# Second attention layer: where the transposed meta probabilities and the query norm sums live in PSUM

## The chip, the cores and the metric

One core of a Trainium2 chip. The metric is the device time of one execution in microseconds; lower is better. The kernel before was timed three times: 2624.48, 2630.35 and 2631.34 us, median 2630.35 us.

## The reference

A two-layer encoder over two sequences ("prompt" and "sample") of 512 tokens with 1024 features; 16 learned meta tokens are put in front of each, so that every sequence has 528 rows. Layer 0 is a gated DeltaNet mixer, layer 1 an attention mixer with compressed queries and keys (MLA). The change lies in layer 1:

```
proj = RMSNorm(h) @ w_in                      # cq 512 | ckv 256 | k_pe 64 | z 2048
q  = RMSNorm(cq)  @ w_uq   -> 16 heads x (128 + 64)
kv = RMSNorm(ckv) @ w_ukv  -> 16 heads x (128 key + 128 value)
q, k = RMSNorm per head over 192, then rotary on the last 64
p = softmax(q k^T / sqrt(192))                # over all 528 keys, the 16 meta keys among them
h = h + (p v * silu(z)) @ w_out               # meta rows dropped from the output
```

All arithmetic is in float32.

## The kernel before

**Arithmetic.** TensorE multiplies rounded operands. Each float32 matrix is split into a high part H (a cast) and a low part L (what the cast lost), and a product is three matmuls, H·H, H·L, L·H (`mm3`, lines 74 to 79; in the trace their lines are L75, L76, L77). The cast is a ScalarE instruction, the subtraction for L is VectorE's or GpSimd's (`sub`, L88). For the 16 meta tokens the three products are folded into one matmul: 80 rows hold H at 0 to 15, a second operand's H at 32 to 47 and L at 64 to 79. These stacked tiles are `pst` (probabilities, two tiles, one per head of a pair) and `vst` (values).

**Work units of layer 1.** 2 sequences x 8 head pairs make 16 units. A unit's preparation (`head`, in the order `pair_k`, `pair_qrope`, `pair_qsplit`, `pair_q` for head 0, `pair_v`, `pair_q` for head 1, `pair_z`) is issued as filling between the tiles of the unit before. Each unit then has 8 attention tiles: 2 heads x 4 query tiles of 128 rows. In `run` the loop over n issues, for each tile, one piece of the next unit's preparation, then `pair_scores` of the next tile, then `pair_out` of this tile.

- `pair_scores` writes 128x528 scores into a PSUM tile S (two banks, two such tiles), VectorE takes the maximum (L1089), ScalarE the exponential (L1093) into P (two SBUF tiles), VectorE scales P (L1096).
- `pair_out` transposes P on TensorE: its 16 meta columns (L1108) into the first 16 partitions of the second bank of S, which is then no longer needed for scores, and its other 512 columns (L1110) into the one `tr` bank. ScalarE copies the meta block twice into pst (L1113, L1114), VectorE subtracts (L88); ScalarE and VectorE split the 512 columns into PTH and PTL (in the trace hnH and hnL, whose memory they use). Query tiles go in pairs: only after the odd one are the output matmuls issued, for 256 columns, into a bank `x`: 12 with the 512 keys' values (L75 to L77), then one with the meta tokens (L1124). VectorE multiplies the result by the gate zs (L1125).
- `pair_q` (L1000 and on) projects the queries of one head, splits them (ScalarE L1009, VectorE qL L1012), and adds up their squares on ScalarE, GpSimd and VectorE (L1011, L1014, L1015). For head 1 it then sums them over the features by four small matmuls (L1020) into a tile of `x`, which VectorE reads (L1022). The key norm sums in `pair_k` (L993) are alike, in a projection bank `pj`.

**PSUM** has eight banks: S 2 x 2, `pj` 2, `tr` 1, `x` 1. A tile is given to its next user when all accesses to it are over.

**Order.** Each engine takes its instructions in order. That order is not the program's text: a list scheduler with a timeline simulation (`schedule_with_timeline_sim=True`) takes, at each step of its simulated time, the ready instruction that stands first in the program, and hands out tiles and semaphores as it goes. Weights are loaded by DMAs of the SP queue.

Of the kernel before, what the change touches and what calls it, by code (L numbers as in the profile page):

```python
# [18 lines left out]
NM = 16  # L19
# [4 lines left out]
class Trunk:  # L24
# [975 lines left out]
    def pair_q(self, u, j):  # L1000
        nc = self.nc
        V, A, G, PE = nc.vector, nc.scalar, nc.gpsimd, nc.tensor
        UQ, cq, sqr, h = self.ins["mla_w_uq"][0], u["c"]["cq"], u["sqr"], u["hs"][j]
        o = self.SIDES[j][0]
        w = self.weights([(0, UQ[:, 192 * h:192 * h + 128])], 4)
        ps = self.project(w, cq, 4, 0, 512)
        qH = self.t("qH", [128, 512], F32R)
        qL = self.t("qL", [128, 512], F32R)
        A.activation(qH, ps, AF.Copy, scale=self.qkg)  # L1009
        sq = self.t("raw", [128, 512])  # L1010
        A.activation(sq, ps, AF.Square)  # L1011
        V.scalar_tensor_tensor(qL, ps, self.qkg, qH.bitcast(F32), op0=ALU.mult, op1=ALU.subtract)  # L1012
        u["q"][j] = qH, qL
        G.tensor_tensor(sqr[o], sqr[o], sq[o], op=ALU.add)  # L1014
        V.tensor_tensor(sqr[o], sqr[o], sq[self.SIDES[j][1]], op=ALU.add)  # L1015
        if j == 0:
            return
        ps = self.p("x", [128, 4, 2])
        for i in range(4):
            PE.matmul(ps[:, i], sqr[:, 128 * i:128 * i + 128], self.two, start=True, stop=True)  # L1020
        t = self.t("qs", [128, 4, 2])
        V.tensor_tensor(t, ps, u["c"]["ce"].unsqueeze(2).to_broadcast([128, 4, 2]), op=ALU.add)  # L1022
        tf = t.rearrange("p a b -> p (a b)")
        self.rsqrt(tf, tf)
        u["qs"] = [t[:, :, j] for j in range(2)]
# [73 lines left out]
    def pair_out(self, u, j, qt, S, P):  # L1099
        nc = self.nc  # L1100
        V, A, G, PE = nc.vector, nc.scalar, nc.gpsimd, nc.tensor
        VH, VL, vst, zs = u["VH"], u["VL"], u["vst"], u["zs"][j]
        pst = self.pst[j]
        vc = slice(128 * j, 128 * j + 128)
        cs = slice(128 * qt, 128 * qt + 128)
        pt = self.p("tr", [128, 4, 128])
        pm = S[0:16, 1, 0:128]
        PE.transpose(pm, P[:, 0:NM], self.ident)  # L1108
        for kt_ in range(4):
            PE.transpose(pt[:, kt_], P[:, NM + 128 * kt_:NM + 128 * kt_ + 128], self.ident)  # L1110
        PTH, PTL = self.PT[qt // 2]
        hc = slice(128 * (qt % 2), 128 * (qt % 2) + 128)
        A.copy(pst[0:16, cs], pm)  # L1113
        A.copy(pst[32:48, cs], pm)  # L1114
        self.sub(V, pst[64:80, cs], pm, pst[0:16, cs])
        A.copy(PTH[:, :, hc], pt)  # L1116
        self.sub(V, PTL[:, :, hc], pt, PTH[:, :, hc])
        if qt % 2 == 0:
            return
        po = self.p("x", [128, 256])  # L1120
        h2 = slice(128 * qt - 128, 128 * qt + 128)
        for kt_ in range(4):
            self.mm3(po, (VH[:, kt_, vc], VL[:, kt_, vc]), (PTH[:, kt_], PTL[:, kt_]), first=(kt_ == 0), last=False)
        PE.matmul(po, vst[:, vc], pst[:, h2], start=False, stop=True)  # L1124
        V.scalar_tensor_tensor(zs[:, h2], po, 0.5, zs[:, h2], op0=ALU.mult, op1=ALU.mult)  # L1125
        if qt == 3:
            nc.sync.dma_start(u["yd"][u["hs"][j]], zs)
# [204 lines left out]
```

## Time and profile before

| | |
|---|---|
| median of three runs | 2630.35 us |
| profiled execution, its own time | 2632.01 us |
| its span, first to last instruction | 2630.3 us |
| mean granted TensorE clock | 0.97 of full speed |
| TensorE busy (matmul) | 2468.7 us, 94% |
| VectorE busy | 1732.9 us, 66% |
| ScalarE busy | 1408.4 us, 54% |
| GpSimd busy | 1166.6 us, 44% |

The profile is one execution. "Busy" of TensorE is the time in which at least one matmul is under way; matmuls overlap, so it is not peak use. The first layer takes the span up to some 1340 us; the attention tiles of the second run from 1540 to 2480 us; the output projection of the last sequence ends the span.

### The profile page before, as it was taken

Reading aid. Unit: us, or ns where it says so; the run is one execution under the profiler, and the core shown is the slowest. Engines: PE = TensorE matmul, PEld = TensorE weight load, DVE = VectorE, ACT = ScalarE, POOL = GpSimd, SP = SyncE. Lnnn points to the kernel's source line nnn. Section 1 sums busy time; section 2 is a strip of 40 time slices with the busy share of each in tenths; the row PEclk is TensorE's granted clock in tenths of the full one; section 3 lists DMA queues with packets and bytes.
Section 4 is the critical chain, followed back from the end, with each engine's and each line's share of the span. In section 5 each row is a group of like instructions: output and inputs, shape, how many; then the busy total and the mean of one; then the engine's idle time right before and its main releaser. Section 6 shows DMA issues by size and latency. Waiting matters only on the chain.

```text
span 2630.3 us, 52159 instructions
## 1 busy us (share of the span) xinstructions
PE 2468.7 (94%) x19083; PEld 2212.1 (84%) x19083; DVE 1732.9 (66%) x3915; ACT 1408.4 (54%) x3424; POOL 1166.6 (44%) x1157
## 2 busy tenths in 40 slices
PE   8889999998999999999989889998998989999999
PEld 7878888888888889888989878888887878888787
DVE  6987888777788867786454256667775567666421
ACT  5545655545455554545545365666656556665432
POOL 6544545432433323323445454555535544554343
PEclk9999999988999999999999999999999999999999
DMA  6544545442333354444465422233332223225575
GB/s 206 176 121 136 153 128 164 136 138 86 112 91 90 113 172 138 133 122 144 127 213 167 130 79 71 73 72 83 90 89 74 81 70 69 77 69 153 167 222 148
DMA packets 453216, 321.06 MB, mean 122 GB/s; under 512 B 134812, under 2 KB 364430, under 8 KB 452960
## 3 DMA queue, kind: packets, MB, share of 16 engines
q1 hardware_dynamic: 452960, 317.73, 41.9%
q8 instruction: 150, 2.46, 0.4%
q14 instruction: 106, 0.87, 0.1%
HBM read 216.02 MB, written 92.67 MB: 117 GB/s over the span
## 4 chain that ended last, share of the span: by engine, by line
PE 58%; DVE 20%; DMA 8%; ACT 6%; issue 4%; POOL 2%; SPq 2%; ACTq 0%; POOLq 0%; DVEq 0%
PE pj L75 12%; PE pj L76 12%; PE pj L77 12%; PE ch L692 2%; PE po L710 2%; DVE acc L374 2%; DVE RL L88 2%; DMA acc<-acc 2%; DVE Yt L504 1%; DVE kq L374 1%; PE ch L703 1%; DVE Y L506 1%; PE lv L552 1%; PE tr L1110 1%; DMA T<-Td 1%
## 5 line engine op out<-in xcount | busy, mean ns | idle before, releaser
L88 POOL TENSOR_TENSOR wl<-wraw,wh 128x512 fp32r<-128x512 f32 (+2 forms) x414 | 547.6, 1325 | 708.8 <-ACT wh L219 675.3
L75 PE MATMUL pj<-hnH,wh 128*128 128x264 f32 (+4 forms) x2080 | 632.8, 305 | 18.9 <-ACT wh L219 5.2
L77 PE MATMUL pj<-hnH,wl 128*128 128x264 f32 (+3 forms) x2080 | 627.6, 303 | 2.6 <-POOL wl L88 1.9
L76 PE MATMUL pj<-hnL,wh 128*128 128x264 f32 (+3 forms) x2080 | 625.2, 301 | 0.7 <-DVE hnL L784 0.6
L219 ACT CAST wh<-wraw 128x512 fp32r<-128x512 f32 (+2 forms) x414 | 248.2, 600 | 346.0 <-PE pj L76 195.8
L75 PEld LDWEIGHTS pj<-hnH,wh 128*128 128x128 f32 (+1 forms) x2080 | 398.9, 192 | 37.6 <-ACT wh L219 5.7
L77 PEld LDWEIGHTS pj<-hnH,wl 128*128 128x128 f32 (+1 forms) x2080 | 398.3, 192 | 17.8 <-POOL wl L88 3.3
L76 PEld LDWEIGHTS pj<-hnL,wh 128*128 128x128 f32 (+1 forms) x2080 | 399.0, 192 | 15.8 <-issue 2.5
L76 PE MATMUL pj<-h2L,wh 128*128 128x512 f32 (+1 forms) x544 | 205.5, 378 | 3.2 <-DVE h2L L88 3.1
L77 PE MATMUL pj<-h2H,wl 128*128 128x512 f32 (+1 forms) x544 | 205.8, 379 | 0.0
L75 PE MATMUL pj<-h2H,wh 128*128 128x512 f32 (+1 forms) x544 | 205.4, 379 | 0.3
L1089 DVE TENSOR_REDUCE mx<-S 128x1 f32<-128x528 f32 x128 | 89.9, 703 | 66.3 <-PE S L1086 65.5
L1093 ACT ACTIVATE P<-S,mx,qs 128x528 f32<-128x528 f32 x128 | 101.5, 793 | 46.6 <-DVE mx L1090 42.7
L76 PEld LDWEIGHTS pj<-h2L,wh 128*128 128x128 f32 x544 | 102.5, 188 | 22.4 <-DVE h2L L88 4.4
L732 POOL TENSOR_TENSOR oa<-oa,ot 128x256 f32<-128x256 f32 (+1 forms) x80 | 69.6, 870 | 114.5 <-DVE ot L730 101.2
L75 PEld LDWEIGHTS pj<-h2H,wh 128*128 128x128 f32 x544 | 102.3, 189 | 20.0 <-DVE cqL L916 0.6
L77 PEld LDWEIGHTS pj<-h2H,wl 128*128 128x128 f32 x544 | 102.7, 189 | 18.1
L374 DVE SCALAR_TENSOR_TENSOR acc<-raw,vec,acc 128x528 f32<-128x528 f32 x128 | 112.4, 881 | 6.7 <-ACT acc L372 5.7
L374 DVE SCALAR_TENSOR_TENSOR kq<-raw,vec,kq 128x528 f32<-128x528 f32 x128 | 105.7, 826 | 8.6 <-ACT kq L372 7.6
L793 DVE TENSOR_TENSOR raw<-raw,pj 128x512 f32<-128x512 f32 (+1 forms) x54 | 31.3, 580 | 120.9 <-PE pj L77 120.7
L1116 ACT CAST hnH<-tr 128x512 fp32r<-128x512 f32 x128 | 74.9, 585 | 61.5 <-PE tr L1110 59.6
L88 DVE TENSOR_TENSOR hnH<-tr,hnH 128x512 fp32r<-128x512 f32 x128 | 88.2, 689 | 19.6 <-ACT hnH L1116 16.1
(483 smaller groups left out, 6789.1 us busy)
## 6 DMA issues: line engine op xcount, KB each, us to landing
wraw<-in_gdn_w_in_dram SPq DMA_DIRECT2D x96, 256.0 KB
wc<-wh SPq DMA_DIRECT2D x96, 256.0 KB
wc<-wl SPq DMA_DIRECT2D x96, 256.0 KB
wh<-wc SPq DMA_DIRECT2D x96, 256.0 KB
wl<-wc SPq DMA_DIRECT2D x96, 256.0 KB
wraw<-in_mla_w_in_dram SPq DMA_DIRECT2D x88, 256.0 KB
wraw<-in_gdn_w_out_dram SPq DMA_DIRECT2D x64, 256.0 KB
wraw<-in_mla_w_out_dram SPq DMA_DIRECT2D x64, 256.0 KB
```

The costliest lines, as they stand in the source:

```text
L75: mm(out, ah, bh, start=first, stop=False)
L76: mm(out, ah, bl, start=False, stop=False)
L77: mm(out, al, bh, start=False, stop=last)
L88: return eng.tensor_tensor(out, a, hi, op=ALU.subtract)
L219: nc.scalar.copy(wh, raw)
L374: nc.vector.scalar_tensor_tensor(acc, raw[:, j:j + T], self.convw(j, u), acc, op0=ALU.mult, op1=ALU.add)
L692: PE.matmul(pc[:n, 0], kq[:, 0, sl], S[d], start=True, stop=True)
L710: PE.matmul(po[:n, 0], kq[:, 1, sl], S[d], start=True, stop=True)
L732: G.tensor_tensor(oa[:n, i], oa[:n, i], t, op=ALU.add)
L1089: V.tensor_reduce(mx, Sv, axis=AX.XY, op=ALU.max, negate=True)
L1093: self.last_P = A.activation(P, Sv, AF.Exp, bias=mx, scale=qs[j][:, qt:qt + 1], accum_out=sm)
L1116: A.copy(PTH[:, :, hc], pt)
```

## The change

In `pair_out` the meta columns of P are transposed into the bank `x` that holds the output accumulation. The bank is taken at the even query tile: columns 0 to 255 are the output, columns 256 to 511 hold the transposed meta columns of the even and of the odd tile. The two casts and the subtraction into pst are left out at the even tile and done at the odd tile for 256 columns at once. The meta matmul becomes the first of the output group instead of the last. In `pair_q` the query norm sums go to a projection bank `pj` instead of `x`.

```diff
@@ pair_q
-        ps = self.p("x", [128, 4, 2])
+        ps = self.p("pj", [128, 4, 2])
@@ pair_out
         pt = self.p("tr", [128, 4, 128])
-        pm = S[0:16, 1, 0:128]
-        PE.transpose(pm, P[:, 0:NM], self.ident)
+        if qt % 2 == 0:
+            u["po"] = self.p("x", [128, 512])
+        po, pm = u["po"][:, 0:256], u["po"][0:16, 256:512]
+        PE.transpose(pm[:, 128 * (qt % 2):128 * (qt % 2) + 128], P[:, 0:NM], self.ident)
...
-        A.copy(pst[0:16, cs], pm)
-        A.copy(pst[32:48, cs], pm)
-        self.sub(V, pst[64:80, cs], pm, pst[0:16, cs])
+        h2 = slice(128 * qt - 128, 128 * qt + 128)
+        if qt % 2:
+            A.copy(pst[0:16, h2], pm)
+            A.copy(pst[32:48, h2], pm)
+            self.sub(V, pst[64:80, h2], pm, pst[0:16, h2])
...
         if qt % 2 == 0:
             return
-        po = self.p("x", [128, 256])
-        h2 = slice(128 * qt - 128, 128 * qt + 128)
+        PE.matmul(po, vst[:, vc], pst[:, h2], start=True, stop=False)
         for kt_ in range(4):
-            self.mm3(po, (VH[:, kt_, vc], VL[:, kt_, vc]), (PTH[:, kt_], PTL[:, kt_]), first=(kt_ == 0), last=False)
-        PE.matmul(po, vst[:, vc], pst[:, h2], start=False, stop=True)
+            self.mm3(po, (VH[:, kt_, vc], VL[:, kt_, vc]), (PTH[:, kt_], PTL[:, kt_]), first=False, last=(kt_ == 3))
```

## Rows read from the trace of the kernel before

**Rows 1.** The page, part 1: busy us, share of the span, instructions.
```profile
PE 2468.7 (94%) x19083; PEld 2212.1 (84%) x19083; DVE 1732.9 (66%) x3915; ACT 1408.4 (54%) x3424; POOL 1166.6 (44%) x1157
```

**Rows 2.** Stage table, 1540 to 2480 us: PE, PEld, DVE, ACT, POOL busy, clock.
```profile
1540.00:2480.00 940.00, 868.90 (x5566) 770.65 (x5565) 606.62 (x1182) 559.48 (x1255) 467.88 (x337) 0.98 0.32 85
```

**Rows 3.** TensorE's waits, 1540 to 2480 us: us in total, times, longest us.
```profile
PE S L1108 <- DVE P L1096: 23.1, 12, 3.6
PE pj L75 <- DVE qL L1012: 15.1, 15, 5.4
PE S L75 <- DVE pst L88: 11.0, 10, 1.4
PE x L75 <- ACT hnH L1116: 7.0, 9, 1.9
PE pj L993 <- POOL sqH L990: 3.9, 7, 1.2
...
PE x L1020 <- DVE sqr L1015: 0.3, 1, 0.3
```

**Rows 4.** Groups by line, 1540 to 2480 us: busy us, mean ns | idle before.
```profile
L1114 ACT CAST pst<-S 16x128 fp32r<-16x128 f32 x128 | 32.6, 255 | 1.5
L1113 ACT CAST pst<-S 16x128 fp32r<-16x128 f32 x128 | 31.8, 248 | 37.6 <-PE S L1108 37.4
...
L1045 ACT CAST vst<-pj 16x256 fp32r<-16x256 f32 x15 | 5.4, 362 | 6.1 <-PE pj L77 4.9
L1046 ACT CAST vst<-pj 16x256 fp32r<-16x256 f32 x15 | 5.4, 360 | 0.2
...
L88 DVE TENSOR_TENSOR pst<-S,pst 16x128 fp32r<-16x128 f32 x128 | 36.1, 282 | 58.6 <-ACT pst L1114 55.6
...
L88 DVE TENSOR_TENSOR vst<-pj,vst 16x256 fp32r<-16x256 f32 x15 | 6.2, 414 | 2.9 <-ACT vst L1046 2.6
```

**Rows 5.** The timeline, 1703 to 1708.5 us: start us, us, instruction, idle before.
```profile
1703.84 0.25 ACT L1113 CAST pst<-S 16x128 fp32r<-16x128 f32 x1
...
1704.72 0.39 PE L75 MATMUL S<-kH,qH 128*128 128x264 f32 x1 [1.34 <-DVE pst L88]
...
1705.40 0.65 ACT L988 ACTIVATE sqH<-kr 64x528 f32<-64x528 f32 x1
...
1705.72 0.28 DVE L88 TENSOR_TENSOR pst<-S,pst 16x128 fp32r<-16x128 f32 x1
...
1706.84 1.32 POOL L990 TENSOR_TENSOR sqH<-sqH,raw 64x528 f32<-64x528 f32 x1 [1.35 <-ACT raw L989]
...
1707.71 0.28 PE L75 MATMUL x<-hnH,hnL 128*128 128x256 f32 x1
```

**Rows 6.** The timeline, 1726 to 1732.2 us, where VectorE is crowded.
```profile
1726.10 3.49 DVE L88 TENSOR_TENSOR RL<-acc,SQ 64x512 fp32r<-64x512 f32 x2
...
1726.82 0.28 PE L1124 MATMUL x<-pst,vst 80*128 80x256 f32 x1
...
1730.92 0.41 DVE L1125 SCALAR_TENSOR_TENSOR zs<-x,zs 128x256 f32<-128x256 f32 x1
...
1731.15 0.27 PE L1108 MATMUL S<-ident,P 128*16 128x128 f32 x1 [2.08 <-DVE P L1096]
```

**Rows 7.** The timeline around two gate projections, from 1688 and from 1741 us.
```profile
1688.08 0.39 PE L75 MATMUL pj<-h2H,wh 128*128 128x512 f32 x1
...
1689.61 0.75 DVE L1012 SCALAR_TENSOR_TENSOR qL<-pj,qkg,qH 128x512 fp32r<-128x512 f32 x1 [0.53 <-ACT raw L1011]
...
1741.50 0.39 PE L75 MATMUL pj<-h2H,wh 128*128 128x512 f32 x1
...
1741.73 0.27 PE L1108 MATMUL S<-ident,P 128*16 128x128 f32 x1
...
1744.22 0.41 DVE L1125 SCALAR_TENSOR_TENSOR zs<-x,zs 128x256 f32<-128x256 f32 x1
1744.55 0.73 DVE L1012 SCALAR_TENSOR_TENSOR qL<-pj,qkg,qH 128x512 fp32r<-128x512 f32 x1
```

## The prediction

> **What bounds the kernel now.** The page's first part comes first: TensorE is busy for 94% of a span of 2630.3 us [rows 1], so a change of some microseconds can only come out of the 6% in which it stands still. The stage table then narrows that to the stretch from 1540 to 2480 us, where the 128 attention tiles of the second layer run (16 head pairs, two heads, four query tiles each): TensorE is busy 868.9 of 940 us at a granted clock of 0.98 of full speed, so 71.1 us are idle there, about 4.7 us for each of the 15 or so head pairs [rows 2]. The change touches nothing outside that stretch and its first few tiles before it. Third, the list of waits says what ends these 71 us [rows 3]: the first transpose of a tile waits for its scaled probabilities P (23.1 us, 12 times); the value projection waits for the split qL of the query projection that sits in the projection bank it wants (15.1 us, 15 times); the scores wait for pst (11.0 us, 10 times); the first output matmul waits for the cast of the transposed probabilities (7.0 us); the key norm sums wait for GpSimd (3.9 us). The reader should see that only the third row names something the change takes away.
>
> The profiled execution took 2632.01 us, 1.7 us around its span; the median of the runs shown is 2630.35, the lowest 2624.48. I make the sum against 2632.0 and carry the difference to 2630.35.
>
> **The change part by part.**
>
> *The meta columns leave the score bank.* Today the transpose of P's 16 meta columns goes into the score tile S itself, so that S stays occupied after the exponential until ScalarE has read those columns twice and VectorE once. The timeline shows the price: ScalarE reads an even tile's meta block from 1703.84 on, VectorE after it, and the scores that want this S start only at 1704.72, after 1.34 us in which TensorE is idle [rows 5]. After the change S is free once the exponential has read it, some microseconds earlier. All ten such waits, 11.0 us, go [rows 3]. What is late next decides how much is kept:
> - Four of the ten (1.34 to 1.36 us each, 5.4 us in all) stand as in rows 5: two tiles of scores follow, and then the key norm sums L993, which already wait for GpSimd's sum [rows 3], here the one at 1706.84. That sum waits for ScalarE's square at 1705.40, which queues behind four pst reads of 0.25 us between 1703.84 and 1705.40 [rows 5]. Two of the four disappear and two become 0.36 us long, so that the square comes 0.28 us earlier if both still go first, 1.0 us if it overtakes them. I take the middle, 0.64, for each: 2.6 us kept of 5.4.
> - Two (0.63 and 1.44 us) are followed within 3 us by waits for P and for qL, which hang on VectorE's own chain: nothing kept.
> - The other four (0.66 to 1.10 us, 3.5 us) are followed by smaller waits of 0.2 to 0.66: I take 2.9.
>
> Together 5.5 us, between 0 and 11.0.
>
> *Half as many, longer reads.* A pair of tiles now costs ScalarE four casts, 2 x (248 + 255) ns = 1.01 us, and VectorE two subtractions, 2 x 282 = 0.56 us. The new shape, 16x256, is in the trace already, for the meta tokens' values: 362 and 360 ns on ScalarE and 414 ns on VectorE [rows 4]. So ScalarE gives back 0.28 us and VectorE 0.15 us for each of 64 pairs, 18 and 9.6 us in all. Neither engine is the bound, so this counts only where a wait of rows 3 hangs on them. For the 12 waits on P I take one dropped subtraction (0.28 us) each, 3.4 us; the ends are 0 and all 23.1. On the other side, in an odd tile the two casts ahead of the cast of the transposed probabilities grow by 0.22 us together, while the meta matmul, now first of the group, fills 0.12 us (20 score matmuls and four transposes take 2.99 us, 1704.72 to 1707.71 [rows 5], 0.12 each). With nine waits in that row of rows 3, 0.1 us each, I take 1.0 us lost (0 to 2.0).
>
> *The output bank is held for two tiles.* The even tile's meta transpose must now wait until VectorE has read the previous pair's output out of x (zs, L1125). Where that read follows at once this costs nothing. Where VectorE is crowded it is late: the last output matmul at 1726.82, the even transpose 0.12 us behind it, but the read only at 1730.92 for 0.41 us [rows 6]. There TensorE stood still anyway until 1731.15, on P. In the next case nothing hides it: even transpose at 1741.73, read from 1744.22 to 1744.63 [rows 7], 2.9 us in the middle of a gate projection of 24 matmuls that waits for no one. TensorE takes its queue in order, so whatever the scheduler put behind the transpose waits with it; but the transpose is needed only at the odd tile's reads, and the scheduler has the rest of the gate projection to put in front. Bounds: 0 to 2.9 us in about half of the 15 head pairs, 0 to 22 us. I take 2.0 in all, near the low end, since the transposes of the other 512 columns, which free P's other part, don't wait for x.
>
> *Query norm sums in a projection bank.* Four small matmuls for each head pair move from x to one of two pj banks. They run after the gate projection today, waited only 0.3 us [rows 3], and their reader is short. If they take their bank only when their input is ready, they cost nothing: 0. If they hold it from their place in the program, the gate projection must take the bank of the second query projection and wait for its qL: 1688.08 to 1690.36 in one head pair, 1741.50 to 1745.28 in the next [rows 7], 2.3 and 3.8 us. That is the upper end, priced below.
>
> *The matmul order.* The meta matmul is first instead of last, the same 64 matmuls. It needs the pst subtraction, which stands at 1705.72 against a first output matmul at 1707.71 [rows 5]: 1.7 us spare; cost 0.
>
> Beside this: the Trainium skill ("PSUM — Partial Sum Buffer", "PSUM bank collisions raise a hardware error") says that two engines must not be in one bank of the same partitions at once, whatever the columns, so the output matmuls can't run while the meta columns beside them are being read. The spare 1.7 us says that the reads are over by then; by the rule alone it is the last of the rivals below.
>
> **The sum:** -5.5 - 3.4 + 1.0 + 2.0 + 0 = -5.9 us: 2626.1 for the profiled execution, 2624.4 beside the median of 2630.35.
>
> **The rivals.**
> - *The freed score bank lets the scheduler run ahead.* Scores of the next tiles can be put where TensorE now waits for P or qL. For it: both waits stand in an in-order queue, and two tiles of scores are 20 x 0.12 = 2.5 us of work. Against it: P has only two buffers, and VectorE, not the scores, is late there (3.49 us of RL in front at 1726.10, rows 6). Half of 23.1 + 15.1 goes: -19, with the sum -25: 2605.
> - *The waits only move.* The 11.0 us reappear at the norm sums, at P and at qL, and nothing else comes: -1, 2629.
> - *The late output read decides, slower.* Place: the even transpose in the gate projection, as at 1741.73 to 1744.63. Price 2.9 us in 7 head pairs, 20 us; with the gains of 8.9 less 1.0 it is +12, 2642. It decides from 1.1 us per such head pair on (7.9 / 7).
> - *The norm sums hold the gate projection back, slower.* 2.3 or 3.8 us, less one tile's ten score matmuls and five transposes put in between (1.9 us at 0.12 each), 0.4 or 1.9: mean 1.2 x 15 = 18; with the sum +12, 2642. For it: nothing in the rows shows a later pj tile taking its bank ahead of an earlier one. Against it: the norm sums today run behind the later gate projection, though in another bank.
> - *The output group waits for the meta reads.* If the pst subtraction were the last thing that this group waits for, its 0.41 us [rows 4] would come on top 64 times, 26 us; with the sum +20, 2650. Against it the 1.7 us spare.
>
> **How the numbers follow.** A median of this kernel's runs can tell about 0.3%, 7.9 us. The forecast has 0.45; its own range is -13 to 0, 2617 to 2630, of which 0.21 lies beyond 7.9 us and 0.24 within. Running ahead 0.18 (all faster), moving waits 0.12 (0.10 same, 0.02 slower), the late read 0.12 (0.10 slower, 0.02 same), the held gate projection 0.10 (0.09 slower, 0.01 same), the last 0.03 (slower). Faster 0.39, same 0.37, slower 0.24. The range runs from the first rival's 2605 to a microsecond beyond the two slower ones' 2642.
>
> **What would show it.** Right: the row "scores wait for pst" gone, pst's ScalarE rows at 64 each of some 360 ns, TensorE's idle time between 1540 and 2480 down from 71 to about 65 us, the norm sums' wait for GpSimd up by some 3 us. Wrong: a new row in which the meta transpose waits for zs with more than some 8 us, a gate projection that waits for qL, or waits for P down by half. What would upset all of it is the scheduler: it orders every engine's queue anew, and a different interleaving in 15 head pairs multiplies each half microsecond by 15.

## The result and the profile after

The kernel after takes 2722.91 us (median of four runs, 2710.01 to 2726.04), the kernel before beside it 2630.22 us (four runs, 2624.48 to 2631.34). The ratio is 1.0336, with a 95% interval of 1.0311 to 1.0362. The prediction said 2624.4 us, with a range from 2605 to 2643: it forecast a gain of 6 us, and the medians show a loss of 92.7.

First the page's busy times of the kernel after (answers to [rows 1]), then its stage table (us, then busy us of PE, PEld, DVE, ACT and POOL with instructions, granted clock, DMA share, GB/s; the first line answers to [rows 2]):

```profile
PE 2502.4 (92%) x19083; PEld 2236.8 (83%) x19083; DVE 1724.2 (64%) x3851; ACT 1392.6 (51%) x3296; POOL 1172.6 (43%) x1157
```

```profile
1540.00:2480.00 940.00, 824.70 (x5070) 727.44 (x5071) 556.71 (x1031) 503.16 (x1045) 443.70 (x314) 0.93 0.27 71
2480.00:2708.00 228.00, 220.29 (x1062) 180.93 (x1060) 70.34 (x119) 81.52 (x150) 87.32 (x67) 0.99 0.61 181
```

The span is 2708.2 us, 77.9 more than before. (The profiled execution is the fastest of the four, 2710.01 us, so the profile shows less than the 92.7 us between the medians.) TensorE executes 19083 matmuls in both kernels, but is busy 33.7 us longer for them (2502.4 - 2468.7), and stands still for 205.8 us instead of 161.6, 44.2 more. So over half of the loss is idle time. The rest fits the granted clock, which was 0.93 of full speed between 1540 and 2480 us and 0.98 before [rows 2]: by the trace's clock records TensorE had its lower level for 122.9 us of that stretch, in 22 pieces, and for 41.0 us, in 9 pieces, in the kernel before. Half of the 82 us between them, 41 us, is an estimate from these records of what that costs if TensorE is busy all the while; 33.7 were measured. The reader should see that the same stretch holds only 5070 matmul records instead of 5566: the work has slipped behind 2480 us.

TensorE's waits in that stretch (us in total, times, longest), against [rows 3]:

```profile
PE x L1110 <- DVE zs L1127: 34.4, 16, 7.5
PE pj L75 <- DVE zs L1072: 34.4, 14, 3.0
PE S L75 <- ACT P L1093: 16.2, 18, 1.1
PE x L76 <- DVE hnH L88: 9.5, 12, 0.8
PE tr L1112 <- DVE hnH L88: 4.4, 6, 0.9
```

The scores' wait for pst is gone, as predicted, and so are the 23.1 us for P and nearly all of the 15.1 us for qL. In their place stand two rows of 34.4 us: the meta transpose into x waits until VectorE has read the last output out of x (zs L1127), and the value projection waits until VectorE has read the second gate projection out of its bank (zs L1072). The reads of pst have the shape and the price that was forecast (whole span, against [rows 4]; busy us, mean ns | idle before):

```profile
L88 DVE TENSOR_TENSOR pst<-x,pst 16x256 fp32r<-16x256 f32 x64 | 26.6, 416 | 10.6 <-ACT pst L1118 8.9
...
L1118 ACT CAST pst<-x 16x256 fp32r<-16x256 f32 x64 | 23.2, 362 | 0.7
...
L1117 ACT CAST pst<-x 16x256 fp32r<-16x256 f32 x64 | 22.6, 354 | 25.9 <-PE x L1110 25.9
```

VectorE's own waits, 1540 to 2570 us, show one row that hardly existed before (4.6 us, once, in the kernel before):

```profile
DVE kr L1055 <- DMA rs<-rkd: 118.2, 15, 15.3
DVE hnH L88 <- ACT hnH L1120: 86.2, 58, 4.8
DVE sm L1094 <- ACT P L1093: 51.6, 52, 4.4
```

In 15 head pairs VectorE stands at the key multiplication kr and waits for the row of inverse key norms, which comes back from DRAM by a DMA of the SP queue. The timeline shows what stands behind it in VectorE's queue, and who waits for that (rows of SP's queue, VectorE and TensorE):

```profile
1904.03 0.32 SPq L998 DMA_DIRECT2D rkd<-rk  x1
...
1910.77 0.34 SPq L955 DMA_DIRECT2D rs<-rkd  x1
...
1915.10 2.43 DVE L1055 TENSOR_TENSOR kr<-kr,rs 128x528 f32<-128x528 f32 x2 [7.47 <-DMA rs<-rkd]
1917.46 0.67 DVE L1072 SCALAR_TENSOR_TENSOR zs<-zs,pj 128x512 f32<-128x512 f32 x1
...
1914.81 0.60 PE L1112 MATMUL tr<-ident,P 128*128 128x128 f32 x4
1918.18 0.58 PE L75 MATMUL pj<-wh,ckvH 128*128 128x256 f32 x1 [2.78 <-DVE zs L1072]
```

That looked like the whole cause. The experiments say that it is not.

One more thing is to be seen in TensorE's timeline, at the norm sums; the last line is of the kernel before:

```profile
1939.35 0.39 PE L1110 MATMUL x<-ident,P 128*16 128x128 f32 x2 [2.05 <-DVE zs L1127]
1941.33 1.57 PE L1020 MATMUL pj<-two,sqr 128*128 128x2 f32 x8 [1.60 <-DVE sqr L1015]
1942.76 0.77 PE L75 MATMUL pj<-h2H,wh 128*128 128x512 f32 x1
...
1944.19 0.63 PE L75 MATMUL pj<-h2H,wh 128*128 128x512 f32 x1
1944.61 0.63 PE L76 MATMUL pj<-h2L,wh 128*128 128x512 f32 x1
...
1948.72 0.40 PE L77 MATMUL pj<-h2H,wl 128*128 128x512 f32 x1
1948.96 0.39 PE L75 MATMUL pj<-h2H,wh 128*128 128x512 f32 x1
...
1949.43 0.39 PE L77 MATMUL pj<-h2H,wl 128*128 128x512 f32 x1
```

```profile
1748.45 0.95 PE L1020 MATMUL x<-two,sqr 128*128 128x2 f32 x8
```

The norm sums (L1020) now stand ahead of the first head's gate projection (h2H, h2L) and wait for their input. In the kernel before they stand behind it: that projection begins at 1741.50 [rows 7], its norm sums at 1748.45. This is so in every head pair of both kernels. The time from one pair's norm sums to the next shows the loss in a compact form: four pairs take 214.3 us before (1641.95 to 1856.25), 53.6 each, and 234.0 us after (1645.37 to 1879.40), 58.5 each. From the first pair's norm sums to the last pair's it is 871.1 us before (1529.65 to 2400.75) and 964.0 after (1517.77 to 2481.76), 92.9 more. Of these 77.9 are left in the span, since the norm sums stand earlier in their pair (the first come 11.9 us earlier) and what follows the last ones is 3.1 us shorter.

### The profile page after: what moved, and what is told of

Its sections match the earlier page's. It is cut to its first block, busy times and chain, and to the rows that moved or that the text cites. A ratio compares the mean times of both kernels' runs of the same rounds, so it can differ in the third digit from the quotient of the medians.

```text
span 2708.2 us, 51962 instructions
## 1 busy us (share of the span) xinstructions
PE 2502.4 (92%) x19083; PEld 2236.8 (83%) x19083; DVE 1724.2 (64%) x3851; ACT 1392.6 (51%) x3296; POOL 1172.6 (43%) x1157
## 5 line engine op out<-in xcount | busy, mean ns | idle before, releaser
L88 DVE TENSOR_TENSOR hnH<-tr,hnH 128x512 fp32r<-128x512 f32 x128 | 88.1, 688 | 88.3 <-ACT hnH L1120 87.3
L1055 DVE TENSOR_TENSOR kr<-kr,rs 128x528 f32<-128x528 f32 x32 | 42.9, 1383 | 119.6 <-DMA rs<-rkd 119.6
L793 DVE TENSOR_TENSOR raw<-raw,pj 128x512 f32<-128x512 f32 (+1 forms) x54 | 31.3, 579 | 120.7 <-PE pj L77 120.6
```

The costliest lines, as they stand in the source:

```text
L88: return eng.tensor_tensor(out, a, hi, op=ALU.subtract)
L793: nc.vector.tensor_tensor(r[:, c0:c0 + chunk], r[:, c0:c0 + chunk], ps, op=ALU.add)
L1055: V.tensor_tensor(kr[:, j], kr[:, j], rs[:, j], op=ALU.mult)
```

## The experiments

Ratios are to runs of the kernel before in the same session, with their 95% interval.

### Which half of the change: e4, e5, e6, e7

```
e5   before, in pair_q:   ps = self.p("x", [128, 4, 2])  ->  self.p("pj", [128, 4, 2])
e4   after,  in pair_q:   ps = self.p("pj", ...)  ->  self.p("x", ...)
e6   after,  in pair_q:   ps = self.p("pj", ...)  ->  self.p("tr", ...)
e7   after,  in pair_out: pst casts and subtraction per tile (16x128), no "if qt % 2"
```

> The kernel before with the query norm sums in a projection bank and nothing else: the score bank still holds the meta tokens' transposed columns, each tile's are read by themselves. Theory Banks (the gate projection of a pair must now take the bank of the second query projection, and every projection after it stands one bank further): most of the loss is here, 2670 to 2720 us, and the value projection waits 25 us or more for the gate's read zs L1072. Theory Interplay (neither half alone gives the scheduler the order of the kernel after): no loss beyond 1%, 2620 to 2655 us. Theory Queue, in the form left by the runs so far (an early kr costs, but kr is early in only 4 of 16 pairs here): a quarter of the early-kr run's loss of 2.7%, about 2650.

> The kernel after, with the query norm sums back in the bank x: only the meta tokens' move, the shared reads and the order of the output matmuls are left of the change. In its order of work the key multiplies stand behind the rope addition again in 14 of 16 pairs, as in the kernel before. Theory Queue: no loss, 2600 to 2645 us, with the scores' wait for pst gone. Theory Banks, held-bank half (the output bank x held for two tiles is what stalls the transposes): the transposes wait 20 us or more for zs and for the norm sums' read, above 2660 us.

> The kernel after with the query norm sums in the bank tr of the transposed probabilities, instead of a projection bank: neither x nor a projection bank is asked for. Theory Banks: the projections keep the banks that they had before, the value projection's wait for zs L1072 stays under 10 us, and the time is that of the meta tokens' move alone (0.9% above before) or less, 2630 to 2665 us. Theory Interplay or anything that the freed score bank does by itself: 2680 us or more.

> The kernel after with the meta columns read per tile again, as in the kernel before (two casts and a subtraction of 16x128 for each tile), but still in the output bank, and the norm sums still in a projection bank. Key multiplies stand late on VectorE here, as in the kernel before. Theory Banks: the norm sums decide, so this loses like the kernel after, 2690 to 2740 us. Theory Merged reads (the longer, later reads of two tiles are what put the order out of joint): back to 2620 to 2660 us.

Measured: the norm sums alone 1.0256 (1.0223 to 1.0289), 2710.13 us; the meta tokens' move alone 1.0089 (1.0057 to 1.0121), 2662.09 us; norm sums in tr 1.0132 (1.0097 to 1.0167), 2673.18 us; reads per tile 1.0346 (1.0316 to 1.0375), 2732.29 us.

The two halves add up: 2.56% and 0.89% make 3.45%, the whole change costs 3.36%. Most of it is the edit that the prediction's sum put at 0. Reading each tile by itself again gains nothing (e7), and without the projection bank 1.3% are left (e6, 8 us above the range of "Banks" and below the other's). The value projection's wait for zs L1072 that "Banks" expected in e5 at 25 us or more is only 10.6, so that row is not how most of the norm sums' cost arises. VectorE stands at the gate's read instead, waiting for ScalarE's function of the gate projection (TensorE's row of e5, 1540 to 2480 us, then VectorE's, 1540 to 2570 us; in the kernel before the row for zs has 32.8 us, 18 times):

```profile
PE pj L75 <- DVE zs L1072: 10.6, 12, 3.6
```

```profile
DVE zs L1072 <- ACT zs L1071: 141.5, 30, 11.7
DVE sm L1094 <- ACT P L1093: 55.5, 81, 1.0
```

In e4 the time is that of "Banks", but not the wait that it named: the meta transposes wait for no output read in that trace. TensorE waits 34.9 us for hnH, 31.3 for qL, and 21.2 us in 12 places for pst, at the first matmul of the output group. That last wait is the prediction's last rival, and this half of the change alone shows it.

### Is it the wait at kr: e1, e2, e3, e16

```
e1   after:  dma_start(rs, u["rkd"]...)  ->  dma_start(rs, rkd of the pair before), at its old place
e2   after:  with self.behind(self.last_q):            # last_q: the newest qL
                 V.tensor_tensor(kr[:, j], kr[:, j], rs[:, j], op=ALU.mult)
e3   before: in head, pair_knorm(u, 0) and (u, 1) ahead of pair_qsplit, which is put behind kr
e16  after:  rs of the pair before, loaded at the top of pair_k;
             each engine's queue chained, from the second layer on, in the order of the kernel after
```

> The kernel after, with one thing changed: the row rs of inverse key norms is loaded from the buffer of the head pair before, which has lain in DRAM for a whole pair, so that VectorE's key multiplies kr no longer wait for the round trip through DRAM. (Left out by it: the key norms of a pair are those of the pair before.) VectorE's order of work is that of the kernel after, instruction by instruction; only the wait goes. Theory Queue (the key multiplies were moved to the head of VectorE's in-order queue, wait there for their DMA, and hold up the reads that free TensorE's banks): the row kr <- DMA rs falls from 118.2 us to under 15, the waits of the value projection for zs L1072 and of the transposes for zs L1127 from 34.4 us each to under 10, the clock in 1540 to 2480 returns from 0.93 to 0.97 or more, and the time to 2600 to 2645 us. Theory Banks (norm sums and gate projection share two banks, and the output bank is held over two tiles, so TensorE waits whatever VectorE's order): the two waits of 34.4 us stay at 20 or more each and the time stays above 2680. Theory Clock (the granted clock fell by itself, without the stalls): waits fall but the clock stays at 0.93, about 2665.

> The kernel after, with an edge that puts the key multiplies kr behind the newest subtraction qL of the query projection on VectorE, where the kernel before has them in most pairs. The whole change stays in: meta tokens in the output bank, one read for two tiles, norm sums in a projection bank. Theory Queue: kr <- DMA rs below 20 us, both waits for zs below 12 each, 2605 to 2645 us, so that nothing or little is left of the 92 us. Theory Banks: both rows keep 20 us or more each, above 2680 us. Theory Held bank (the even tile's meta transpose waits for the output read, as a rival of the prediction had it): the transposes' wait for zs L1127 stays at 20 us while the value projection's goes, 2640 to 2670.

> The kernel before, with nothing of the change, but the key multiplies kr of both heads written ahead of the rope addition L964 of the same pair and the addition ordered behind them. Theory Queue: the change's loss appears without the change: kr <- DMA rs at 80 us or more, the clock of 1540 to 2480 below 0.96, and 2670 to 2730 us. Theory Banks: the order of VectorE's queue alone costs little, under 2645. A third outcome, between 2645 and 2670, says that the early multiplies cost half, and the banks that the change shares out the rest.

> The first experiment again, without its fault (there the load of rs stayed behind the swap's DMAs and came as late as before): the kernel after, every engine held in its own order from the second layer on, with rs loaded from the pair before, straight after that pair's last reader and free of this pair's DMAs. (The key norms of a pair are again those of the pair before.) Theory Queue (the 118 us in which VectorE stands at kr, with the gate's and the output's reads behind it, carry the loss): kr <- DMA rs under 15 us, TensorE's two waits for zs (34.4 us each) under 10 us, 2650 us or less. Theory Sums first (the norm sums ahead of the gate projection and the order that follows from that carry the loss, and the wait at kr is its consequence, since kr stands early in that order): the rows for kr and zs fall, but other waits take their place, 2690 to 2730 us. A result between, 2650 to 2690, gives the wait at kr a share of the loss.

e1: 1.0368 (1.0328 to 1.0408), 2734.98 us, but it says nothing of the theory: the row is still there.

```profile
DVE kr L1060 <- DMA rs<-rkd: 120.9, 15, 13.9
```

The load stayed behind the swap's DMAs in the SP queue (issued at 1936.91 us, the swap from 1934.42 to 1936.87), so the edit did not take away the wait that it was made for.

e2: 1.0353 (1.0315 to 1.0391), 2732.08 us. With kr behind qL the wait at kr is out of the list and nothing is gained. VectorE stands at the gate's read instead, and TensorE's waits go to other rows (VectorE's first, 1540 to 2570 us, then three of TensorE's, whole span):

```profile
DVE zs L1073 <- ACT zs L1072: 122.5, 30, 12.8
```

```profile
PE S L75 <- ACT P L1094: 31.8, 26, 1.7
PE tr L1113 <- DVE hnH L88: 19.6, 14, 2.3
PE pj L75 <- DVE qL L1012: 15.7, 7, 3.6
```

e3: 1.0270 (1.0234 to 1.0305), 2709.86 us, with kr <- DMA rs at 60.3 us. An early kr in the kernel before, with all that the scheduler changes for it, does cost 2.7%, though it waits less than the 80 us that were expected.

e16 is the clean one: the order of the kernel after, with the wait at kr gone from VectorE's list altogether (in its place VectorE waits 87.3 us at the gate's read). 1.0274 (1.0244 to 1.0305), 2704.07 us. TensorE's first row shows that the waits only moved:

```profile
PE x L1114 <- DVE zs L1131: 41.2, 15, 4.5
PE S L76 <- ACT P L1097: 15.0, 18, 1.2
```

The value projection's wait for the gate is gone with it, the transposes' wait for the output read has grown from 34.4 to 41.2 us, and 2.7 of 3.4% remain. The most striking row of the profile carries some 0.6% (3.36 - 2.74, measured in two sessions; the kernel after held in its own order without the edit was not timed); "Queue" falls as the main cause, and the result is inside the range of "Sums first". That the same move of kr costs 2.7% in e3 is no contradiction: there the order of everything else changes as well.

### The place of the norm sums: e9, e10, e11, e17

```
e9   before: with self.behind(u["N"]):  self.pair_z(u, 0)      # N: the last norm sum, still in x
e10  before: norm sums to "pj", and their code moved out of pair_q to behind pair_z(u, 0) in head
e11  after:  the same move
e17  e10 again, in another session
```

> The kernel before, with nothing of the change, but the gate projection of a pair's first head ordered behind the query norm sums on TensorE; these stay in bank x. Theory Sums first (a projection bank is handed out in the order of the program, so the norm sums in it must run before the gate projection, which covered their wait for VectorE and GpSimd until now): this order alone costs what the norm sums alone cost, 2680 to 2730 us. Theory Bank (the bank that the sums occupy, not their place, is what costs): under 2655 us.

> The kernel before with the query norm sums in a projection bank, but written in the program after the first head's gate projection, so that they may take their bank after it. Theory Sums first: most of the 2.6% that the norm sums cost alone comes back, 2625 to 2660 us. Theory Bank: 2680 us or more.

> The whole change, with the query norm sums written after the first head's gate projection in the program. Theory Sums first: what is left is the cost of the meta tokens' move alone (0.9%), 2640 to 2675 us. Theory Bank: 2700 us or more. Theory Fit (the order of the kernel before happens to fit the chip's real durations, and any other order costs 1 to 3%): anything between, above 2660.

> The norm sums in a projection bank, written after the gate projection, and nothing else of the change: the version that came out ahead of the kernel before (ratio 0.9974, between 0.9957 and 0.9992), in another session. If it is really ahead: 0.995 to 0.999. If that was chance: an interval that reaches beyond 1.0.

Measured: e9 1.0318 (1.0290 to 1.0346), 2722.08 us; e10 0.9974 (0.9957 to 0.9992), 2630.16 us; e11 1.0126 (1.0090 to 1.0162), 2674.19 us; e17 0.9976 (0.9959 to 0.9994), 2622.40 us.

This settles which edit the larger part hangs on. e9 has nothing of the change but one order, the norm sums ahead of the gate projection, and loses 3.2%. e10 has the projection bank and the old order, and loses nothing. So the bank costs nothing; what costs is that a projection bank is given out in the order of the program, in which the norm sums of `pair_q` stand ahead of `pair_z`. Written behind `pair_z`, they take the bank after it. In the whole change that one move gives back 2.1 of the 3.4% (e11).

The traces of all runs can be sorted by this one place. The norm sums stand ahead of the first head's gate projection in all 16 pairs in the kernel after, e1, e2, e5, e7, e9 and e16, and all seven cost 2.6 to 3.7%. They stand behind it in e4, e6, e8, e10 to e15, e17 and e18, which cost 1.3% at most, but for e8 with 2.7%; e3, where they come ahead of its last few matmuls in most pairs, costs 2.7% as well. So this place is enough for such a loss, but it is not the only way to one.

Stage and waits of e9, then of e10:

```profile
1540.00:2480.00 940.00, 824.10 (x5154) 727.97 (x5153) 553.85 (x1102) 527.83 (x1182) 430.01 (x317) 0.93 0.27 72
```

```profile
PE S L1108 <- DVE P L1096: 25.6, 10, 3.0
PE S L75 <- DVE pst L88: 22.2, 15, 2.4
PE pj L75 <- DVE qL L1012: 15.1, 14, 2.9
```

```profile
1540.00:2480.00 940.00, 876.00 (x5588) 772.70 (x5588) 593.17 (x1188) 566.60 (x1261) 467.52 (x338) 0.98 0.31 85
```

```profile
PE S L1109 <- DVE P L1097: 18.0, 13, 2.7
PE pj L75 <- DVE qL L1012: 12.1, 14, 3.9
PE S L75 <- DVE pst L88: 7.7, 15, 0.7
```

e9's stage row is that of the kernel after, 0.93 and all, without one edit of the change: TensorE is idle for 115.9 of the 940 us, where it was 71.1 [rows 2]. Its largest waits have the same names as before [rows 3], with pst's at twice its size; they make up 62.9 of the 115.9 us, and the rest is spread over rows of 9 us and less. Four pairs take 229.1 us in e9, 57.3 each (1653.45 to 1882.53), and 209.7 us in e10, 52.4 each.

### How the place costs: e12, e18

```
e12  before: zat = 0 if i == 15 else 2   ->   0 if i == 15 else 3
e18  before: TensorE's queue chained in its own order, but the 24 matmuls of each gate projection
             gathered at the place of the thirteenth
```

> The kernel before with no edit in content: the second head's gate projection is written one tile later in the program (at the fourth tile of a pair instead of the third), which moves 12 to 24 matmuls in each pair's order and nothing else by much. Theory Fit: slower by 0.7% or more, 2660 us or above, though nothing is computed or waited for in another way. Theory Sums first: norm sums still stand behind the gate projection, so nothing of the 2.6% appears: 2620 to 2655 us.

> The kernel before with TensorE's queue held in its own order, but for one thing: the 24 matmuls of each of the 32 gate projections, which stand in 2.3 pieces on average there (5 of 32 in one piece; 31 of 32 in the kernel after, 25 with the norm sums ordered first), are gathered at the place of their thirteenth. The norm sums stay behind them, in bank x. The other engines are ordered anew by the scheduler. Theory Cover (the pieces of the gate projection stand between the transposes and cover the waits for VectorE and ScalarE there; in one piece they don't): 2670 to 2720 us. Theory Place (it is the place of the norm sums ahead of the gate projection, not the pieces, that costs): under 2650 us.

e12: 1.0018 (0.9997 to 1.0040), 2643.20 us. e18: 1.0005 (0.9982 to 1.0027), 2641.46 us beside 2640.64.

e12 speaks against the idea that the order of the kernel before merely fits the chip and any other costs 1 to 3%: this one moves half of the gate projections by a tile (590 of their 1248 matmuls stand one or two tiles later in the trace) and costs next to nothing. e18 answers what looked like the mechanism. In the built orders 5 of the 32 gate projections stand in one piece before, 31 after, 25 in e9 and 5 in e10, so that cover for the transposes seemed to be what is lost. Gathered into one piece, with the norm sums left behind them, they cost nothing: "Cover" is wrong.

### What is left, 1.3%: e8, e13, e14, e15

```
e8   before: pm = S[0:16, 1, 0:128]  ->  pm = self.p("x", [16, 128])   # S free early, x not held
e15  e10 and e8 together
e14  e11, and in pair_scores the matmuls behind the last transpose (L1112) of two tiles before
e13  e11, each engine's queue chained in the order of the kernel before in 15 of 16 pairs; the even
     meta transpose beside the odd one, the norm sums ahead of the next pair's key projection
```

> The kernel before with one edit: the meta columns are transposed into an x tile of their own for each tile, so that the score bank is free after the exponential, while the output group takes x afterwards as before; norm sums in x as before. It tests the freed score bank by itself. Theory Freed bank (scores run ahead, and the order that the scheduler makes of it is worse): slower, 2650 us or more, with the scores' wait for pst gone. Theory Banks: no harm in the freed bank, 2615 to 2645 us.

> The kernel before with the norm sums in a projection bank and written late, and the meta columns transposed into an x tile of each tile's own, given back after its reads: the score bank is free after the exponential, but x is not held over two tiles and the reads are not shared. Theory Freed bank: the freed score bank alone gives the worse order, 2660 us or more. Theory Held bank: without the hold nothing is lost, 2620 to 2650 us.

> The whole change with the norm sums written late, and one more edge: the scores of a tile may be issued on TensorE only behind the transposes of the tile two before it, where the score bank that was still being read held them until now. Theory Freed bank (scores run ahead of the transposes and crowd the tiles of a pair together): part of the 1.3% comes back, 2640 to 2660 us, and the transposes' wait for hnH (21.7 us without the edge) falls below 12. Theory Held bank (the even tile's meta transpose has to wait for the output read, and the order suffers from that): no change, 2665 to 2685 us.

> The whole change with the norm sums written late, and every engine's queue held in the order of the kernel before by ordering edges, in 15 of the 16 head pairs; only what the banks forbid is moved (the even tile's meta transpose stands beside the odd tile's, the norm sums ahead of the next pair's first key projection). This is the prediction's own premise. Theory Order (nothing in the change costs time, the orders that the scheduler makes of it do): the prediction's sum holds, 2615 to 2640 us beside a kernel before of 2637, and the row of scores waiting for pst is gone. Theory Bank (the output bank held over two tiles, or the shared reads, cost by themselves): the 1.3% of the whole change with late norm sums stays, 2660 to 2680 us.

Measured: e8 1.0274 (1.0249 to 1.0300), 2713.39 us; e15 1.0092 (1.0058 to 1.0125), 2656.19 us; e14 1.0053 (1.0032 to 1.0073), 2643.54 us; e13 1.0092 (1.0067 to 1.0117), 2654.90 us.

e14 shows one part: with the scores held behind the transposes of two tiles before, 0.7 of the 1.3% come back. The transposes' wait for hnH is out of the list, as "Freed bank" had it, but it has moved on to the output group (e11's two rows for hnH, then e14's largest):

```profile
PE tr L1113 <- DVE hnH L88: 21.7, 11, 2.3
PE x L76 <- DVE hnH L88: 5.5, 9, 2.4
```

```profile
PE x L77 <- DVE hnH L89: 25.3, 26, 2.0
```

What is shorter is the idle time in all, 80.7 of the 940 us where e11 has 99.3: the scores' wait for the exponential (18.0 us) is gone and the one for qL falls from 14.0 to 2.1. The clock is 0.98 again, where e11 has 0.95. So the wait that the change removed was also a brake. e15 lies between its two theories: with a score bank that is free early and no bank held over two tiles, 0.9% are lost. It doesn't separate the two, since its meta tiles ask for x as well: TensorE waits 14.2 us for pst's reads before the output group may have x, and 9.7 us for x at the meta transposes. What e8 loses beyond that was not taken apart.

e13 is the prediction's own premise, every queue in the order of before, and it lies between the two theories, 26.7 us above the kernel before beside it (stage, then waits):

```profile
1540.00:2480.00 940.00, 862.49 (x5421) 767.01 (x5420) 583.17 (x1096) 529.93 (x1103) 457.23 (x330) 0.95 0.30 81
```

```profile
PE x L1111 <- DVE zs L1128: 16.7, 6, 3.6
PE x L1111 <- DVE P L1097: 11.4, 7, 4.3
PE pj L993 <- POOL sqH L990: 9.4, 9, 2.9
```

The scores' wait for pst is gone, as the sum had it, and the one for P is half of what it was, 11.7 us less where the sum took 3.4. Against that the meta transposes wait six times, 2.8 us each, for the output read, and the key norm sums wait 5.5 us more for GpSimd. Over the whole profile TensorE's idle time is 165.2 us (2653.2 - 2488.0), only 3.6 above before; its busy time is 19.3 us longer. So the change in the old order has next to no more idle time and a lower clock: 0.95 in the stretch, where before has 0.98 [rows 2]. That the fewer but longer stalls at the held bank lowered it is a reading of these rows and was not tested; nor was the kernel before timed with every queue held (e18 holds TensorE's alone, and costs nothing).

## Why the prediction was wrong, point by point

- **"The meta columns leave the score bank", -5.5 us.** The edit does what it says: the row is gone, and pst's reads take 354, 362 and 416 ns where 362, 360 and 414 were forecast. But the sum counted the wait as lost time only. It held the scores behind the transposes, and e14 shows that such a hold is worth 0.7% (1.26 less 0.53, in two sessions), some 19 us: more than the whole row.
- **"Query norm sums in a projection bank", 0.** This is the step that failed. The prediction put two conditions: they take their bank when their input is ready (0), or from their place in the program (the rival "norm sums hold the gate projection back", chance 0.10). The second holds: the norm sums run ahead of the gate projection in all 16 pairs of the kernel after. By itself that place costs 69 us (e5), and the same bank costs nothing where the sums are written behind the gate projection (e10, e17). The prediction's evidence against it was that the sums "run behind the later gate projection, though in another bank"; in e10 and e5 that very order turns on the place in the program.
- **The price of that rival, 18 us.** Measured alone it is 69 us (2710.13 - 2640.82, e5) and, as a pure order, 85 us (2722.08 - 2636.97, e9). So the rival had the right place and the wrong wait. It priced a gate projection that waits for qL; in the kernel after that row has 0.3 us, once. The norm sums' own wait for their input (sqr) is small too: 1.6 us at their matmuls and 5.5 at their weight loads, between 1540 and 2480 us. The 4 us more of each pair are spread over many rows (in e5 the wait for hnH L1116 grows from 7.0 to 18.0 us, and the value projection's for the gate's read from nothing to 10.6; in e9 the wait for pst from 11.0 to 22.2), so a price from one wait could not find them.
- **"The output bank is held for two tiles", 2.0.** Mis-sized; the rival's price of 20 us (2.9 us in 7 pairs) was the better one: 16.7 us in 6 places in the old order (e13), 34.4 us in 16 places in the kernel after. Its place was right too, the even transpose ahead of the output read.
- **"Running ahead" as a gain, -19.** Scores did run ahead, and the waits for P and qL did fall from 23.1 and 15.1 us to next to nothing. They were replaced by the two rows for zs, and by 16.2 us in which the scores wait for the exponential to give up their bank. Half of the mechanism was right, and its sign was wrong.
- **"The output group waits for the meta reads", 26 us.** No: between 1540 and 2480 us this group's first matmul waits 1.4 us for pst in 7 places, and its weight load 5.0 us in 13. With the norm sums back in x (e4) it does wait, 21.2 us in 12 places, so the 1.7 us spare that spoke against it belonged to one order.
- **The clock** stood in no term. 33.7 of the profile's 77.9 us are the same 19083 matmuls busy for longer, at a clock of 0.93 in the stretch.
- **"What would upset all of it is the scheduler".** It stood in the last paragraph and not in the sum or in the range. With queues free to change, each of five edits (e3, e5, e8, e9 and the whole change) costs 2.6 to 3.4%, four others 0.9 to 1.3% (e4, e6, e11, e15), and two nothing (e10, e12).

What stays open: by which chain the norm sums' place costs 3%. It is not the bank (e10), not their own wait (1.6 and 5.5 us), not the gate projection's pieces (e18), and only to about a fifth the wait at kr (e16). In e5, e9 and e2 VectorE stands for 113 to 142 us at the gate's read (1540 to 2570 us), where it stands for 33 in the kernel before and 32 in e10; in the kernel after it stands there for 32 too, but for 118 at kr, and once that wait is taken away (e16) for 87. So a gate projection that comes late for VectorE's queue fits; it was not tested by itself.

## What to carry to other kernels

When a tile moves to another pool, look up which tiles of that pool stand next to it in the program and what then runs ahead of what: here a move worth -0.2% with its code one call later was +2.6% without. A wait that disappears may have been the brake that kept work spread out, so ask what will be issued in its place before its microseconds are counted as won. Where a scheduler writes the queues, chain them in the old order and time that: it separates what an edit costs from what its new order costs, and a large new wait row in the profile is a suspect until a run without it has been timed.

## What the runs showed of the hardware

Behind the waits of 2.05 and 1.60 us at 1939.35 and 1941.33 above, the granted clock was at its lower level for some 6 us (two stretches of the kernel after):

```profile
1942.80:1948.40 5.60, 5.60 (x14) 4.40 (x15) 1.16 (x5) 1.44 (x3) 1.64 (x1) 0.50 0.00 0
1948.80:1950.00 1.20, 1.20 (x7) 0.98 (x6) 0.00 (x0) 0.00 (x0) 1.03 (x1) 1.00 0.00 0
```

The gate projection's matmuls come 0.42 us apart in the first stretch (1944.19, 1944.61), at 1.2 GHz, and 0.24 apart in the second (1948.72, 1948.96), at 2.4. The twelve between 1943.33 and 1948.45 take 5.12 us, some 2.3 us more than at the higher level, so 3.65 us of waiting cost about 6 in all here. I put the 33.7 us down to such stretches; no run took the stalls away one by one.

The key multiplication takes 0.70 us (median) before and 1.77 us after. In the kernel after, GpSimd's multiplication by the same rs is released by the same DMA and begins beside it:

```profile
1915.14 1.83 POOL L1058 TENSOR_TENSOR acc<-kpr,rs 128x528 f32<-128x528 f32 x1 [0.94 <-DMA rs<-rkd]
1916.92 1.74 POOL L88 TENSOR_TENSOR wl<-wraw,wh 128x512 fp32r<-128x512 f32 x1
```

VectorE's two multiplications run from 1915.10 to 1917.53, 2.43 us for 1.4 us of work, and end 0.6 us after GpSimd's, which takes 1.83 us (its median is 1.79 in the kernel after and 1.50 before; the shortest take 1.29). The Trainium skill ("SBUF — State Buffer", "Who interferes with whom") says that a VectorE instruction with two SBUF inputs and a GpSimd instruction that reads SBUF shut each other out of a shared port; the trace agrees.
